# Linear attention's six projections as seven products of halves, x kept outside, states in a ring; one side of the FFN in two pieces

## The chip, the cores and the metric

The kernel runs on one core of a Trainium2 chip. TensorE (PE) multiplies: a stationary operand of 128 x 128 is loaded (PEld), a moving operand of up to 512 columns streams past it, and the sums land in PSUM. VectorE (DVE) and ScalarE (ACT) work on SBUF and PSUM, GpSimd (POOL) on SBUF; SyncE (SP) and POOL issue the transfers from and to HBM. Each engine works through its own queue in order. The metric is the device time of one execution in microseconds (us), the median of several runs.

## The reference, cut to what matters

A trunk of four layers on 512 rows of 1024 columns: S5, gated linear attention, differential attention, S5, each followed by an FFN. Everything is float32. The second layer's mixer:

```python
def gla_mixer(h, w_in, w_a2, b_a, norm_g, w_o):
    proj = h @ w_in
    q, k, v, g, a_lo = jnp.split(proj, [512, 1024, 2048, 3072], axis=-1)
    log_a = jax.nn.log_sigmoid(a_lo @ w_a2 + b_a) / 16
    cum = jnp.cumsum(log_a in chunks of 64, axis=2)
    tot = cum[:, :, -1]
    k_dec = k * jnp.exp(tot[:, :, None] - cum)
    upd = jnp.einsum('bnchk,bnchv->bnhkv', k_dec, v)
    state = exp(tot)[..., None] * state + upd        # over the 8 chunks, 4 heads
    o = jnp.einsum('bnchk,bnhkv->bnchv', q, states)
    o = o * rsqrt(mean(o * o) + eps) * norm_g        # per head
    return (o * silu(g)) @ w_o

x = x + gla_mixer(rmsnorm(x, norm_mix[1]), ...)
x = x + swiglu_ffn(rmsnorm(x, norm_ffn[1]), w_gate_up[1], w_down[1])
```

`q` and `k` have 512 columns each, `v` and `g` 1024 each, `a_lo` has 16. So `h @ w_in` is six blocks of 512 columns and a narrow one.

## The kernel before

**Products.** Each float32 product is made of three: an operand is split into a rounded high part and the low rest (`high`, a cast on ACT, L405; `low`, a subtraction on DVE, L413), and high x high, high x low and low x high are summed in PSUM (`mm3`, L433 to L435). A weight block is loaded by SP into one of three staging tiles (`wst`) and split into one of five tiles (`whl`).

**FFN blocks.** The gate and up products of the FFN already use seven products instead of eight (`seven_block`, `seven_product` with the matmul at L576). Rows of h are halved (th), its columns are halved (the depth), and a pair of 256-column weight blocks makes the 2 x 2 outputs. The left sides are 11, 12, 22 (quarters of h, transposed) and 1 to 4 (sums and differences of quarters); each lies split in `place`. The right sides are weight quarters 11, 21, 22 and sums of them: two sums are made by a load that adds to what is there (POOL, L612), two by an addition on DVE (L669). A product is 24 matmuls of 256 columns. The products are called one, five, six, two, seven, three, four; `a` and `c` are banks of the tag acc, `d` (product two) is one of the tag s.

**Sides.** `Sides` holds h for such a layer: the four quarters F in one tile, the sides 11 and 12 behind one another in another (L166 to L168, at 48 and 2112 of 4160 elements), the others opened in the layer's own pool. `Left` holds h split as a whole (`hT`), for layers that use plain products. Either is filled in the tail of the stage before: `take` multiplies x by the gain, `put` transposes, `keep` stores.

**The order.** `hand` says which engines follow the order in which the program is written; the others are ordered by a planner with a cost model, earliest written first among what it holds to be ready. An FFN begins with a start written out for all engines (`plan`, L755 to L770), in which two blocks run interleaved while the norm's factors and the sides are being made. The other blocks are the planner's. Linear attention has only TensorE written out.

**Linear attention before** (`gla`, L1894). q comes from `gemm_a4` (weights stationary, so that q is transposed). The low-rank gate (L1950) follows. Then five plain blocks by `gemm_b` (L437): v0, k, v1, g0, g1, each with four steps of 24 matmuls of 512 columns. Between the steps other work is put: `decays` (L1956: the gate's second product, and Abs, Exp, Ln on ACT), `later` (the suffix sums and their Exp into `kd`), `totals` (L1971), the recurrence `updates` and `readout` (L1986, L2013), and the transposes of the output (L2049). All eight states of two heads are kept in tiles of [128, 8, 256]. A readout takes squares on ACT and a root on POOL (L524). x stays in SBUF. The output projection (L2100) fills the next FFN's sides.

Of the kernel before, what the change touches and what calls it, by code (L numbers as in the profile page):

```python
# [22 lines left out]
P = 128  # L23
# [13 lines left out]
DIFF_LAYER = 2  # L37
LAMBDA_INIT = 0.8 - 0.6 * math.exp(-0.3 * DIFF_LAYER)

# [114 lines left out]
class Sides(Left):  # L154
# [5 lines left out]

    def room(self):
        F = self.tr.hp.tile([P, 4, 4, 256], F32, tag="hT", name="halves")
        self.whole = F
        self.F = {(0, 0): F[:, 0], (1, 0): F[:, 1], (0, 1): F[:, 2], (1, 1): F[:, 3]}

        two = self.tr.hp.tile([P, 4096 + 64], F32R, tag="hT", name="sides")  # L166
        at = lambda n: two[:, n : n + 2048].rearrange("p (z k n) -> p z k n", z=2, k=4)
        self.place = {"11": at(48), "12": at(2112)}  # L168
        self.heads = []

    def quarter(self, q, half, b):
        return self.w[
            q * 512 : (q + 1) * 512, half * FFN_HIDDEN + b * 256 : half * FFN_HIDDEN + (b + 1) * 256
        ].rearrange("(a p) n -> p a n", p=P)
# [15 lines left out]
    def parts(self, name, src, ks=slice(0, 4)):  # L190
        o = self.place[name][:, :, ks]
        self.tr.nc.scalar.copy(o[:, 0], src)
        self.tr.nc.vector.tensor_tensor(o[:, 1], src, o[:, 0].bitcast(F32), op=ALU.subtract)
# [132 lines left out]
class Trunk:  # L326
# [110 lines left out]
    def gemm_b(self, stat, w, nk, c0, evac, k0=0, tail=0, between=(), ahead=None, jobs=False, behind=None):  # L437
# [25 lines left out]
        if tail:  # L463
# [4 lines left out]
            for t in range(NT):  # L468
# [6 lines left out]
                evac(t, accs[t])  # L475

# [89 lines left out]
    def seven_product(self, side, w, bank, first, hl=None):  # L566
# [4 lines left out]
        for j in range(2):  # L571
            c = slice(j * P, (j + 1) * P)
            o = bank[:, j * 256 : (j + 1) * 256]
            for k in range(4):
                for n, (x, y) in enumerate(((0, 0), (0, 1), (1, 0))):
                    mm(  # L576
                        o, hl[:, x, k, c], side[:, y, k], start=first and not (j or k or n),
                        stop=k == 3 and n == 2, skip_group_check=True,
                    )

    def seven_block(self, fp, slots, left, wgu, b, turn, na):
# [4 lines left out]
        A = left.place  # L586
# [52 lines left out]
        def product(side, name, bank, first):  # L639
            self.seven_product(A[side], W.get(name), bank, first, H.pop(name, None))  # L640
# [81 lines left out]
    def ffn(self, l, left, after=None, turn=False, aside=None, small=None):  # L722
# [7 lines left out]
        with self.tc.tile_pool(name=f"ffn{l}", bufs=1, reuse_waits="tile") as fp:  # L730
# [40 lines left out]
            for step in plan.split():  # L771
                name, _, n = step.partition(":")
                if n:
                    f["ab".index(n)][name]()
                elif name[-1] in "ab":
                    word = next(w for w in ("split", "add", "high", "low") if name.startswith(w))
                    w = name[len(word) : -1]
                    f["ab".index(name[-1])][word]({"S": "1", "F": "1"}.get(w, w))
                elif name in ("finish", "diag", "spread", "rows"):
                    getattr(left, name)()  # L780
                elif name == "square":
                    left.square(NT - 1, 1)
                elif name == "flush":
                    self.flush()
                elif name == "turn":
                    r = self.turn_x(left.r) if turn else r
                else:
                    word = next(w for w in ("total", "high", "low") if name.startswith(w))
                    getattr(left, word)(name[len(word) :])
# [10 lines left out]
            for nb in (4, 4, 3) if na == 4 else (3, 3, 3, 2):  # L800
# [25 lines left out]
                if b0 + nb == 11:  # L826
                    nxt = (Chunks if turn else Last if l == 3 else Left)(self, after)
                for d in range(2):
                    tail = 4 if d == 1 and b0 + nb == 11 else 0
                    self.gemm_b(stat, wd, 2 * nb, d * 512, self.add_x(d, nxt, r), k0=2 * b0, tail=tail, jobs=jobs,  # L830
                                behind=None if d or l == 0 else dict(self.last))
# [1061 lines left out]

    def gla(self, l, left, after):  # L1894
# [4 lines left out]
        self.hand(mybir.EngineType.PE)  # L1899
        with self.tc.tile_pool(name="gla", bufs=1) as p:  # L1900
            self.edge(p, 64)
            big = lambda name, tag="g8", bufs=5: p.tile([P, 4, 512], F32, tag=tag, name=name, bufs=bufs)
            late = lambda name: big(name, "g8late", 3)
            oT = [p.tile([P, 2, 4, SEQ], F32R, name="oT0"), None]
            qT = late("qT")
            T = lambda tag, bufs=2: p.tile([P, 512], F32, tag=tag, name=tag, bufs=bufs)

            mask = p.tile([P, P], F32, name="mask")
# [7 lines left out]
            ind = p.tile([P, 2], F32, name="ind")  # L1916
# [3 lines left out]
            ng = p.tile([P, D], F32, name="ng")  # L1920
            nc.sync.dma_start(ng[:], i["gla_norm"][0].partition_broadcast(P))
            wa2 = p.tile([P, 512], F32, name="wa2")
            nc.gpsimd.memset(wa2[:], 0.0)
# [3 lines left out]
            wal = self.wp.tile([P, KT, 16], F32, tag="wst", name="wal", bufs=3)  # L1927
            nc.sync.dma_start(wal[:], w[:, 3072:3088].rearrange("(a p) n -> p a n", p=P))
            walr = p.tile([P, KT, 32], F32R, name="walr")
            nc.scalar.copy(walr[:, :, :16], wal[:])  # L1930
            v.tensor_tensor(walr[:, :, 16:], wal[:], walr[:, :, :16].bitcast(F32), op=ALU.subtract)

            hT = left.hT
# [606 lines left out]
```

## Time and profile before

| what | value |
|---|---|
| median of the 3 runs shown | 2264.95 us (2261.33 to 2266.5) |
| the profiled execution, time | 2264.01 us |
| its span, first to last instruction | 2262.1 us |
| TensorE clock granted, mean | 0.996 |
| linear attention's q begins, last plain block before the output projection ends | 579.8 us, 748.1 us |

The page lists, for groups of instructions, busy time, mean duration of one, and the idle time of the engine in front of them with what ended most of it. A stage row gives for a stretch of time how long each engine was busy. A wait row names who waited for whom, in us, how often, and the longest. In a timeline the first number is the start, the second the duration of what was merged into the row; matmuls overlap, so the time that one takes is read from start to start.

### The profile page before, as it was taken

To read this page: it belongs to the slowest core of one execution; us is meant where nothing else is said; L and a number is where in the kernel's file an instruction comes from. 1 tells how busy PE (TensorE), PEld (TensorE's weight loads), DVE (VectorE), ACT (ScalarE), POOL (GpSimd) and SP (SyncE) were. 2 spreads that over 40 slices of the span, in tenths; PEclk is the share of its full clock that TensorE was granted. 3 is DMA by queue.
4 is the path that set the end of the run, shared out by engine and by line. 5 is a ranking of instruction groups with operands and counts; after the bars stand their busy time and mean duration, and the time that the engine had idled before them with its cause. 6 is when DMAs were issued, how large, how long until landed. Compare 5 with 4: busy or idle time off the path is not lost.

```text
span 2262.1 us, 37360 instructions
## 1 busy us (share of the span) xinstructions
PE 2191.7 (97%) x14967; PEld 1963.9 (87%) x14967; DVE 1580.2 (70%) x2411; ACT 1111.5 (49%) x1773; POOL 317.9 (14%) x432
## 2 busy tenths in 40 slices
PE   6999999999999999999999999999999899999998
PEld 5888889989777799998988888989998788989997
DVE  9955878776535488776745676967766965957675
ACT  8534535444443365564435676644544234635443
POOL 4301141431000010100002231101000000101000
PEclk9999999999999999999999999999999999999999
DMA  4356666763322566765237465985641546766632
GB/s 89 65 170 167 172 159 176 173 172 100 106 76 74 149 158 178 180 172 154 94 137 149 100 152 138 237 212 134 174 99 50 153 146 155 198 160 161 165 75 75
DMA packets 295527, 319.92 MB, mean 141 GB/s; under 512 B 70141, under 2 KB 235289, under 8 KB 295226
## 3 DMA queue, kind: packets, MB, share of 16 engines
q1 hardware_dynamic: 232730, 235.79, 34.5%
q0 software_dynamic: 62624, 81.75, 19.5%
q8 instruction: 118, 1.93, 0.4%
q14 instruction: 55, 0.45, 0.1%
HBM read 285.62 MB, written 16.65 MB: 134 GB/s over the span
## 4 chain that ended last, share of the span: by engine, by line
PE 48%; DVE 3%; ACT 2%; issue 1%; DMA 1%; POOL 0%; DVEq 0%; POOLq 0%; ACTq 0%; SPq 0%
PE a L576 10%; PE acc L433 8%; PE acc L435 8%; PE acc L434 8%; PE c L576 5%; PE d L576 3%; PE y L1481 1%; PE op L2323 1%; PE s L2290 1%; DVE whl L413 1%; PE acc L2378 1%; ACT whl L405 1%; PE V L1445 1%; PE tp L116 0%; DMA wst<-in_ffn_w_gate_up_dram 0%
## 5 line engine op out<-in xcount | busy, mean ns | idle before, releaser
L413 DVE TENSOR_TENSOR whl<-wst,whl 128x1024 fp32r<-128x1024 f32 x272 | 331.6, 1223 | 276.9 <-ACT whl L405 276.2
L405 ACT CAST whl<-wst 128x1024 fp32r<-128x1024 f32 x272 | 284.6, 1051 | 339.7 <-PE acc L435 250.3
L576 PE MATMUL a<-side,whl 128*128 128x256 f32 x3168 | 383.9, 277 | 6.9 <-DVE whl L413 6.0
L576 PEld LDWEIGHTS a<-side,whl 128*128 128x128 f32 x3168 | 371.0, 188 | 9.2 <-DVE whl L413 6.7
L433 PE MATMUL acc<-whl,act 128*128 128x512 f32 x704 | 276.4, 393 | 1.7 <-DVE g L621 1.2
L434 PE MATMUL acc<-whl,act 128*128 128x512 f32 x704 | 275.0, 391 | 0.0
L435 PE MATMUL acc<-whl,act 128*128 128x512 f32 x704 | 274.9, 390 | 0.0
L576 PE MATMUL c<-side,whl 128*128 128x256 f32 x2112 | 255.2, 277 | 3.3 <-DVE whl L413 3.3
L576 PEld LDWEIGHTS c<-side,whl 128*128 128x128 f32 x2112 | 247.0, 188 | 4.2 <-DVE whl L413 4.1
L413 DVE TENSOR_TENSOR whl<-slot,whl 128x1024 fp32r<-128x1024 f32 x105 | 127.7, 1221 | 67.3 <-ACT whl L405 66.9
L433 PEld LDWEIGHTS acc<-whl,act 128*128 128x128 f32 x704 | 132.5, 188 | 30.8 <-DVE g L621 1.7
L435 PEld LDWEIGHTS acc<-whl,act 128*128 128x128 f32 x704 | 132.4, 188 | 27.6
L405 ACT CAST whl<-slot 128x1024 fp32r<-128x1024 f32 x105 | 110.0, 1052 | 92.5 <-PE acc L435 41.2
L434 PEld LDWEIGHTS acc<-whl,act 128*128 128x128 f32 x704 | 132.4, 188 | 26.4 <-issue 0.2
L576 PE MATMUL d<-sides,whl 128*128 128x256 f32 x1056 | 133.7, 283 | 2.5 <-ACT whl L405 2.5
L576 PEld LDWEIGHTS d<-sides,whl 128*128 128x128 f32 x1056 | 128.9, 191 | 3.3 <-ACT whl L405 3.3
L576 PE MATMUL a<-sides,whl 128*128 128x256 f32 x1056 | 129.3, 278 | 1.2 <-DVE whl L413 1.2
L433 PE MATMUL acc<-whl,hT 128*128 128x512 f32 x320 | 128.6, 402 | 0.0
L576 PEld LDWEIGHTS a<-sides,whl 128*128 128x128 f32 x1056 | 125.2, 188 | 2.4 <-DVE whl L413 1.4
L435 PE MATMUL acc<-whl,hT 128*128 128x512 f32 x320 | 125.3, 392 | 0.0
L434 PE MATMUL acc<-whl,hT 128*128 128x512 f32 x320 | 125.3, 391 | 0.0
L612 POOL DMA_DIRECT2D wst<-in_ffn_w_gate_up_dram x44 | 57.0, 1295 | 443.9 <-DMA wst<-in_ffn_w_gate_up_dram 222.7
(456 smaller groups left out, 3935.1 us busy)
## 6 DMA issues: line engine op xcount, KB each, us to landing
wst<-in_ffn_w_gate_up_dram SPq DMA_DIRECT2D x88, 512.0 KB, 4.6
wst<-in_ffn_w_down_dram SPq DMA_DIRECT2D x88, 512.0 KB, 4.4
slot<-in_ffn_w_gate_up_dram SPq DMA_DIRECT2D x69, 512.0 KB, 5.7
wst<-in_ffn_w_gate_up_dram POOLq DMA_DIRECT2D x44, 512.0 KB, 6.2
halves<-in_ffn_w_gate_up_dram SPq DMA_DIRECT2D x42, 512.0 KB, 5.0
wst<-in_s_w_glu_dram SPq DMA_DIRECT2D x32, 512.0 KB, 4.9
wst<-in_gla_w_in_dram SPq DMA_DIRECT2D x24, 512.0 KB, 3.7
wst<-in_diff_w_qkv_dram SPq DMA_DIRECT2D x24, 512.0 KB, 4.6
```

What stands on the lines that cost most here:

```text
L405: self.last["high"] = self.nc.scalar.copy(hl[:, 0], w[:])
L413: self.last["low"] = self.nc.vector.tensor_tensor(hl[:, 1], w[:], hl[:, 0].bitcast(F32), op=ALU.subtract)
L433: mm(out, lh, rh, start=first, stop=False)
L434: mm(out, lh, rl, start=False, stop=False)
L435: self.last["mm"] = mm(out, ll, rh, start=False, stop=last)
L576: mm(o, hl[:, x, k, c], side[:, y, k], start=first and not (j or k or n), stop=k == 3 and n == 2, skip_group_check=True,)
L612: nc.gpsimd.dma_start(w[:], left.quarter(*plus, b), accum_op=ALU.add)
L1445: mm(V[kk][z][:, bs(b)], inm[:, z, bs(b)], U[:, bs(b)], start=True, stop=True)
L1481: mm(yb[:, b], q[:, j, b], om[:, j // 2, bs(b)], start=False, stop=j == 3)
L2290: nc.tensor.matmul(ss[m][:], qs[:, m, ts], ks[:, m, z], start=z == 0, stop=z == 1)
L2323: nc.tensor.matmul(op[:, 0], aT[:, kt], vall[0][:, kt, j * P : (j + 1) * P], start=kt == 0, stop=kt == 3)
L2378: nc.tensor.matmul(o, stat(k, x, t), hl[:, y, a], start=not (k or t % 2 or n), stop=k == KT - 1 and n == 2, skip_group_check=True,)
```

## The change

All six projections of the linear attention become blocks of seven products. `GLA_COLS` names the first 256 of each block's columns: the order is now q, v0, k, v1, g0, g1, and a pair is the two halves of one block. The layer's h is a `Sides` with its own columns.

- The FFN 0 tail now prepares the sides, two split weights and total 3 (`gla_ahead`, `middle`), all engines in written order; the first half of x is stored to HBM there, the second at the start of the layer, both by POOL.
- q and v0 run as an interleaved start with the FFN's plan, less its gate steps and with `gates` (the narrow weight) and `negative` (the factors with the sign changed). q is made with weights stationary; the others with `held`, where the side is stationary and the weight moves, so rows come out as rows. Their evacuation is in pieces of 256 columns, scaled by the norm's factor.
- The low-rank gate uses sides 11, 12, 1 and 22.
- k, v1, g0, g1 follow as `block`, seven steps each: `decays` after the first product of k, `totals` after the third, `later` after the first of v1, the recurrence of heads 0 and 1 in v1, that of 2 and 3 in g0, the transposes of the first output half in g1.
- The tile of x serves as `work`: the low-rank gate, a ring of three pairs of states, and scratch. After the last readout x is loaded back by POOL.
- `later` writes its Exp to scratch and multiplies it into `kd` on DVE; silu works in place on the gate.
- In `Sides`, for all layers, 11 moves to 560, and 12 is held as k = 0 at 0 and k = 1 to 3 at 2608, each split by its own two instructions.

```diff
+GLA_COLS = (0, 1024, 512, 1536, 2048, 2560)
...
-        at = lambda n: two[:, n : n + 2048].rearrange("p (z k n) -> p z k n", z=2, k=4)
-        self.place = {"11": at(48), "12": at(2112)}
+        at = lambda n, k=4: two[:, n : n + 512 * k].rearrange("p (z k n) -> p z k n", z=2, k=k)
+        self.place = {"11": at(560)}
+        self.split12 = [(slice(0, 1), at(0, 1)), (slice(1, 4), at(2608, 3))]
...
+        pieces = self.split12 if name == "12" else [(slice(0, 4), self.place[name])]
+        for ks, o in pieces:
+            self.tr.nc.scalar.copy(o[:, 0], src[:, ks])
+        for ks, o in pieces:
+            self.tr.nc.vector.tensor_tensor(o[:, 1], src[:, ks], o[:, 0].bitcast(F32), op=ALU.subtract)
...
+                    two = (row(x, k)[:, c], hl[:, y, k]) if held else (hl[:, x, k, c], row(y, k))
...
                     if l == 0:
+                        nxt = Sides(self, after, None, i["gla_w_in"][0], lambda half, b: GLA_COLS[b] + half * 256)
...
+    def gla_ahead(self, left):
+        self.xkept = self.dp.tile([SEQ, D], F32, name="xgla")
+        left.ahead(2)
+        self.nc.gpsimd.dma_start(
+            self.xkept[:].rearrange("(t p) c -> p t c", p=P)[:, :, :512], self.x[:, :, :512]
+        )
...
+            nf = self.sp.tile([P, NT], F32, name="nf", bufs=1)
...
+            nc.gpsimd.dma_start(xd[:, :, 512:], self.x[:, :, 512:])
...
+            plan = """
+                split21a one:a split21b square flush one:b total1 one_out:a finish high1 low1 total2 split1a high2 low2
+                negative one_out:b two:a two:b split1b high3 two_out:a five:a add22a highSa two_out:b lowSa five_out:a
+                five:b add22b highSb diag lowSb low3 split3a six:a spread five_out:b rows six:b six_out:a split3b seven:a
+                six_out:b total4 split22a high4 low4 seven:b seven_out:a split22b three:a seven_out:b gates
+                add21a high22 low22 three:b highFa add21b lowFa highFb lowFb four:a four:b three_out:a three_out:b
+                four_out:a four_out:b
+            """
...
+            work = self.xp.tile([P, NT, D], F32, tag="x", name="work")
+            flat = whole(work)
+            aT, wa2 = flat[:, :512], flat[:, 512:1024]
+            ring = flat[:, :3072].rearrange("p (s z c n) -> p s z c n", s=3, z=2, c=2)
...
                 for t, bank in enumerate(four("suf")):
                     nc.tensor.matmul(row(bank), mask[:], la[:, t], start=True, stop=True)
-                    nc.scalar.activation(kd[:, t], row(bank), AF.Exp, scale=1.0 / 16.0)
+                    e = T()
+                    nc.scalar.activation(e, row(bank), AF.Exp, scale=1.0 / 16.0)
+                    v.tensor_tensor(kd[:, t], kd[:, t], e, op=ALU.mult)
...
+            def block(b, out, between):
+                between = iter(between)
+                s = self.seven_quarters(slots, left, b, True, out, self.acc)
+                for y in ("direct", "room1", "room22", "room21", "summed"):
+                    s[y]()
+                def step(*names):
+                    for n in names:
+                        s[n]()
+                    next(between, lambda: None)()
+                step("one", "one_out")
+                step("five", "five_out")
+                s["add"]("22")
+                step("six", "six_out")
+                step("two", "two_out")
+                step("seven", "seven_out")
+                step("three", "three_out")
+                s["add"]("21")
+                step("four", "four_out")
...
             pause = lambda: None
-            values(0, (decays, pause, pause, later))
-            self.gemm_b(stat, w, KT, 512, evac_k, between=(totals,))
-            values(1, core(0))
...
-            gated(0, core(1))
...
-            gated(1, (first, *(lambda t=t: turned(0, (t,)) for t in (1, 2, 3))))
+            block(2, Rows(kd), (decays, pause, totals))
+            vs[1] = room("D", "v1")
+            block(3, Rows(vs[1]), (later, *core(0)))
+            block(4, gated(0, room("C", "gate0")), core(1))
+            self.x = self.xp.tile([P, NT, D], F32, tag="x", name="x")
+            nc.gpsimd.dma_start(self.x[:], xd)
+            oT = [[room("D", "oT0"), room("A", "oT0")], None]
+            turns = [pause] + [lambda t=t: turned(0, (t,)) for t in range(NT)]
+            block(5, gated(1, room("C", "gate1")), turns)
```

373 lines of the change are left out of this document (256 added, 117 removed).

## The prediction

> **What bounds the kernel now.** I read the page first (busy time, the costliest groups), then TensorE's waits and the busy time by stage around the linear attention, then the timeline of TensorE, ScalarE and VectorE there.
>
> ```profile
> span 2262.1 us, 37360 instructions
> PE 2191.7 (97%) x14967; PEld 1963.9 (87%) x14967; DVE 1580.2 (70%) x2411; ACT 1111.5 (49%) x1773; POOL 317.9 (14%) x432
> L576 PE MATMUL a<-side,whl 128*128 128x256 f32 x3168 | 383.9, 277 | 6.9 <-DVE whl L413 6.0
> L576 PE MATMUL d<-sides,whl 128*128 128x256 f32 x1056 | 133.7, 283 | 2.5 <-ACT whl L405 2.5
> ```
> ```profile
> 580.00:800.00 220.00, 218.24 (x1038) 169.88 (x1037) 94.85 (x150) 86.08 (x141) 13.15 (x20) 0.99 0.36 101
> 800.00:870.00 70.00, 66.67 (x574) 65.86 (x573) 65.65 (x76) 45.24 (x60) 8.78 (x7) 1.00 0.73 187
> 870.00:1110.00 240.00, 239.55 (x1690) 222.91 (x1689) 181.09 (x292) 128.28 (x182) 19.92 (x20) 1.00 0.57 151
> ```
> ```profile
> PE acc L435 <- DVE oT L530: 1.0, 2, 0.7
> PE tp L116 <- DVE hh L94: 0.8, 1, 0.8
> ```
> ```profile
> PE a L576 <- DVE whl L413: 1.7, 1, 1.7
> PE c L576 <- DVE whl L413: 1.1, 1, 1.1
> PE d L576 <- ACT whl L405: 0.4, 1, 0.4
> ```
>
> The stage rows give wall time, then busy time of PE, its weight loads, DVE, ACT and POOL. Linear attention fills 580 to 800: TensorE stands only 1.8 us, in the output projection (first list of waits), while DVE works 94.85 of 220 us. So only fewer TensorE cycles can shorten this stage, and DVE has room to pay for them. The next FFN shows the price: its first two blocks of seven products (800 to 870) keep DVE at 65.65 of 70 us, and TensorE waits 3.3 us for split weights (second list). After that, with DVE at 181.09 of 240, nothing waits.
>
> **1. The products.** Starts on TensorE:
>
> ```profile
> 540.99 2.88 PE L576 MATMUL a<-side,whl 128*128 128x256 f32 x24
> 543.71 3.02 PE L576 MATMUL d<-sides,whl 128*128 128x256 f32 x24
> 546.57 2.90 PE L576 MATMUL a<-side,whl 128*128 128x256 f32 x24
> ...
> 597.66 0.39 PE L433 MATMUL any<-hT,whl 128*128 128x512 f32 x1
> ...
> 600.38 0.39 PE L433 MATMUL any<-hT,whl 128*128 128x512 f32 x1
> ```
>
> Twelve 512-wide matmuls take 600.38 - 597.66 = 2.72 us, one 0.2267. A product of 24 matmuls of 256 columns takes 543.71 - 540.99 = 2.72 too. A projection was 96 matmuls of 512, 21.8 us; it becomes 7 products, 19.0. Six of them: 130.6 - 114.2 = **-16.3 us**. (The gate's low-rank product goes from 16 matmuls of 512 to 32 of 256: nothing.) Were each second product to run like d (2.86), 0.8 less is gained.
>
> **2. The written-out start (q and the first values).** It is the FFN's order of steps, so I price it by that start's 3.3 us. Against it: the gate's scaling and the activations' splits are gone, and the low-rank product follows, which asks nothing of DVE; so the second and third waits should fall away. For a loss: the FFN 0 tail ahead of it is only 48 matmuls (10.9 us), in which DVE must now also split two weights ahead and form total 3. **+2.5 us**, ends 1.5 and 6.
>
> **3. The wait at the totals.** This is where I expect the gain to leak.
>
> ```profile
> 613.39 0.59 ACT L1961 ACTIVATE e<-z 128x512 f32<-128x512 f32 x1
> 614.00 1.28 ACT L1962 ACT_TABLE_LOAD   x1
> 615.29 0.63 ACT L1962 ACTIVATE e<-e 128x512 f32<-128x512 f32 x1
> ...
> 629.07 1.28 ACT L1963 ACT_TABLE_LOAD   x1
> 630.36 0.63 ACT L1963 ACTIVATE e<-e 128x512 f32<-128x512 f32 x1
> 630.90 1.98 ACT L405 CAST whl<-wst 128x1024 fp32r<-128x1024 f32 x2
> ```
> ```profile
> 631.02 0.69 DVE L1964 SCALAR_TENSOR_TENSOR la<-z,e 128x512 f32<-128x512 f32 x1 [3.20 <-ACT e L1963]
> ```
> ```profile
> 612.20 3.60 PE L1959 MATMUL z<-wa,aT 128*128 128x512 f32 x8
> 615.23 0.80 PE L433 MATMUL acc<-whl,hT 128*128 128x512 f32 x1
> ...
> 640.89 3.73 PE L1975 MATMUL dps<-ind,la 128*128 128x2 f32 x32
> 644.48 0.78 PE L433 MATMUL acc<-whl,hT 128*128 128x512 f32 x1
> ```
>
> The decays' last `la` is done at 631.71, 19.5 us after their matmuls begin (612.20). Before, the totals (L1975) came 28.7 us after that beginning. In the new order, written out for TensorE, the decays stand behind the first product of the keys' block, and the totals two products later: 615.23 - 612.20 = 3.0 us of decays, five 2.72, six 2.72, so 8.5. The totals take 644.48 - 640.89 = 3.6 us, tile by tile, and without a wait would end at 12.1. Their last quarter (0.9) cannot start before 19.5 and ends at 20.4: a wait of 8.3. One cast of 1.05 us (two in 1.98 at 630.90) that the planner slips between the exponentials adds itself: **+9 us**. What is queued behind the chain on ScalarE is the cast of six's weight, and the products after it. At most five split weights can be held, now 5 x 2.72 = 13.6 us of work, where each covered 5.44 before. Ends: 0 (decays finished in time) and 16 (six's cast behind the whole chain: chain 18.8, cast 1.05, low part 1.22, six 2.72, totals 3.6 = 27.4, and 1 of restart, less 12.1). The row at 644.48 shows that the first product after the totals starts slowly; it does so in both kernels, so nothing is added.
>
> A page speaks against this place: the Trainium skill, ScalarE: Activation LUTs, section "What ACT_TABLE_LOAD costs", puts 1.38 us of drain behind each 1.283 us load. By it the chain's eight loads would take 11 us more and the change would lose. Here the next activation starts at 615.29, where the load of 614.00 ends, so I give the rule no weight.
>
> **4. The three blocks with the recurrence.** DVE, per block: seven low parts, two sums of weights, six half-width evacuations, and the recurrence, the key decay, the gate's product or the splits of the turned output.
>
> ```profile
> L413 DVE TENSOR_TENSOR whl<-wst,whl 128x1024 fp32r<-128x1024 f32 x31 | 37.9, 1224 | 80.7 <-ACT whl L405 80.7
> L2008 DVE SCALAR_TENSOR_TENSOR st<-st,dec,upd 128x256 f32<-128x256 f32 x28 | 12.2, 475 | 0.0
> L2036 DVE SCALAR_TENSOR_TENSOR on<-op,rs,ng 128x256 f32<-128x256 f32 x16 | 7.0, 480 | 3.1 <-POOL rs L524 3.1
> L2061 DVE TENSOR_TENSOR on<-on,e 128x512 f32<-128x512 f32 x8 | 5.3, 688 | 4.4 <-ACT e L2060 4.3
> L530 DVE TENSOR_TENSOR oT<-oTp,oT 128x512 fp32r<-128x512 f32 x8 | 5.3, 683 | 0.1
> ```
> ```profile
> 667.95 1.14 PE L1998 MATMUL upd<-v,kd 64*128 64x256 f32 x8
> 669.02 0.50 PE L433 MATMUL acc<-whl,hT 128*128 128x512 f32 x1
> ...
> 674.68 1.08 PE L2022 MATMUL op<-st,qT 128*64 128x256 f32 x8
> 675.70 1.14 PE L1998 MATMUL upd<-v,kd 64*128 64x256 f32 x8
> ```
>
> Low parts and sums are 9 x 1.22 = 11.0, evacuations 6 x 0.48 = 2.9, a recurrence 16 x 0.475 + 8 x 0.48 + small = 12, the rest 4 x 0.69 = 2.8. Values block: 28.7 us of DVE against 19.0 + 3.0 (the suffix sums, of the decays' form) + 4 x (1.07 + 1.02) = 30.4 of TensorE. First gate block: 28.7 against 27.4. Second: 11.0 + 2.9 + 2.8 + 2.7 = 19.4 against 20.5. Together 76.8 against 78.3. Where DVE set the pace (800 to 870) it was busy 94%; 76.8 / 0.94 = 81.7, so **+3 us**; ends 0 (five weights split ahead in the wait of part 3) and 15 (the rival below).
>
> **5. Side 12 in two pieces.** In the FFNs the product of side 12 (d) takes 546.57 - 543.71 = 2.86 us, all others 2.72. The page's means, 283 and 277 ns, say so for all 1056 of d's matmuls, 44 products. Every one of its 24 matmuls starts about 6 ns late, so this is no wait, and the place of the side is what differs. If both pieces run like the other sides: 44 x 0.14 = 6.2 us won. Three of the four k land exactly 2048 elements behind side 11, which is fast; of the fourth I know nothing. **-4.7 us** (three quarters); ends -6.2 and +6.2, as side 11 moves too and could catch d's pace. The two extra instructions per side (an extra start on ACT and DVE) lie in the tail of the stage before: nothing.
>
> **6. x outside.** The two stores stand on POOL's queue ahead of the start and behind its loads; the work tile needs them some 40 us later (14 products of 2.72 and the low-rank product).
>
> ```profile
> xkeep<-x POOLq DMA_DIRECT2D x1, 2048.0 KB, 12.0
> ```
>
> A store of all of x landed in 12.0 us. The way back begins when the last readout frees the tile, and the first sum into x comes after the last gate block (20.5) and most of the first output half (21.8): hidden, 12 if that cover were gone. SP's and POOL's loads of the last block are issued beside it. States in a ring of three, qT's scaling and silu apart: same operations, DVE time counted above. The 1.8 us of waits in the output projection stay.
>
> **Sum:** -16.3 + 2.5 + 9 + 3 - 4.7 = -6.5. The profiled execution took 2264.0 us (span 2262.1 and 1.9 around it), 0.9 under the median 2264.95 of the runs shown. 2264.0 - 6.5 = **2257.5 us**.
>
> **Rivals.**
> *POOL's queue paces DVE (slower).* POOL computes the readouts' roots; before, it had nothing else in those blocks, and DVE still waited 3.1 us for it (L2036). Now each block puts two accumulating loads into the same queue.
>
> ```profile
> L612 POOL DMA_DIRECT2D wst<-in_ffn_w_gate_up_dram x44 | 57.0, 1295 | 443.9 <-DMA wst<-in_ffn_w_gate_up_dram 222.7
> ```
>
> In the FFNs POOL stood before 44 of these 443.9 us, 10 us each, half of it on the plain load's landing. A root behind one stops DVE's queue, and with it the low parts that TensorE wants. Four of the eight readouts held 5 us each, less the 1.5 that is spare each time: +14, 2271.5. It decides once DVE waits over 11 us for POOL there. Against: the planner may put roots first.
>
> *The totals do not wait* (decays early enough, or the planner groups the loads): -9, 2248.5. Against: 17.6 us of ScalarE chain are in the trace.
>
> *Side 12 does not do what it says* (pieces as slow as before): 2262.2.
>
> **Chances.** Forecast 0.43 (2251 to 2262 by its own terms), POOL's queue or six's cast behind the chain, with a saturated DVE, 0.25, no wait at the totals 0.17, side 12 without effect 0.15. The range takes in the second and third: 2246 to 2271. A measurement of this kernel tells about 0.2%, 4.5 us, from no change. Faster: 0.40 of the forecast, 0.17 of no wait, 0.01 of side 12 = 0.58; same: 0.03 of the forecast, 0.12 of side 12, 0.03 of POOL's queue = 0.18; slower: 0.22 of POOL's queue, 0.02 of side 12 = 0.24.
>
> **What would show it.** Right: products at 2.72 us in the attention; a wait at L1975's totals of 8 to 10 us behind `la`; DVE above 90% from the values block on, with TensorE's waits there under 5 us; d in the FFNs nearer 2.72 than 2.86. Wrong: a totals wait under 3 or over 12; waits of DVE for POOL's roots above 11 us; other side products slower than 2.72 (their addresses may shift by a small new tile); x's return named before a sum into x.

## The result, and the profile after

| kernel | median | lowest to highest |
|---|---|---|
| before | 2263.14 us | 2261.04 to 2266.5 |
| after | 2290.1 us | 2288.71 to 2292.56 |

After to before: 1.0114, 95% interval 1.0102 to 1.0126. The forecast was 2257.5 us, range 2246 to 2271: 32.6 us too low, and on the wrong side.

The page of the kernel after (span, busy time, groups: busy us, mean ns of one, idle before):

```profile
span 2287.0 us, 38452 instructions
PE 2214.7 (97%) x15415; PEld 1998.0 (87%) x15415; DVE 1638.5 (72%) x2487; ACT 1143.8 (50%) x1837; POOL 340.1 (15%) x447
L592 PE MATMUL a<-side,whl 128*128 128x256 f32 x3240 | 406.4, 281 | 6.9 <-DVE whl L426 4.4
L447 PE MATMUL acc<-whl,act 128*128 128x512 f32 x704 | 279.3, 397 | 0.0
L592 PE MATMUL c<-side,whl 128*128 128x256 f32 x2160 | 270.1, 281 | 2.8 <-DVE whl L426 2.8
L592 PE MATMUL d<-sides,whl 128*128 128x256 f32 x1080 | 132.5, 278 | 2.6 <-ACT whl L418 2.6
```

The groups of TensorE before, where the prediction did not show them:

```profile
L434 PE MATMUL acc<-whl,act 128*128 128x512 f32 x704 | 275.0, 391 | 0.0
L576 PE MATMUL c<-side,whl 128*128 128x256 f32 x2112 | 255.2, 277 | 3.3 <-DVE whl L413 3.3
```

TensorE is as busy as before (97%), and the waits for VectorE's split weights in front of the products on the opened sides have become smaller (4.4 and 2.8 us, for 6.0 and 3.3). The FFNs' matmuls themselves are slower: products on the opened sides 281 ns for 277, the FFN's output matmuls 397 for 391. Only d gained (278 for 283). The timelines of one group of products show it, first before, then after (start, duration of the merged row). A group is the run of products between two output stretches, and an output stretch is the run of the FFN's output matmuls behind it.

```profile
419.20 2.99 PE L576 MATMUL a<-sides,whl 128*128 128x256 f32 x24
422.02 2.99 PE L576 MATMUL c<-side,whl 128*128 128x256 f32 x24
424.85 2.99 PE L576 MATMUL a<-side,whl 128*128 128x256 f32 x24
427.68 3.04 PE L576 MATMUL d<-sides,whl 128*128 128x256 f32 x24
430.55 2.90 PE L576 MATMUL a<-side,whl 128*128 128x256 f32 x24
```
```profile
420.80 2.90 PE L592 MATMUL a<-sides,whl 128*128 128x256 f32 x24
423.54 3.00 PE L592 MATMUL c<-side,whl 128*128 128x256 f32 x24
426.38 3.00 PE L592 MATMUL a<-side,whl 128*128 128x256 f32 x24
429.22 2.94 PE L592 MATMUL d<-sides,whl 128*128 128x256 f32 x24
431.99 3.00 PE L592 MATMUL a<-side,whl 128*128 128x256 f32 x24
```

Start to start, before: 2.82, 2.83, 2.83, 2.87, and behind these nearly all 2.72, product d aside (2.86). After: 2.74, 2.84, 2.84, 2.77, 2.83, and this pattern repeats to the end of the group. The three blocks of this group (21 products) take 57.93 us before (419.20 to the first output matmul at 477.13) and 59.13 after (420.80 to 479.93); an output stretch of FFN 2 takes 43.54 and 44.81. Summed over the four FFNs, from the first start of each stretch to the first of the next, the groups of products cost 16.8 us more and the output stretches 10.8 more. Together that is 27.6 us; less the 2.7 that the linear attention gained (below), it is the 24.9 us by which the spans of the two profiles differ.

The linear attention gained. From its first product to the first output matmul: 168.24 us before (579.83 to 748.07), 165.51 after (584.49 to 750.00). TensorE's longest waits there (total, times, longest), and VectorE's wait for POOL's roots:

```profile
PE dps L2229 <- DVE la L2216: 3.6, 1, 3.6
PE op L2269 <- DVE work L2256: 0.9, 2, 0.7
```
```profile
DVE on L2283 <- POOL rs L539: 3.9, 7, 1.1
```

The gain is 2.7 us where some 2 were forecast for the attention's terms, and the longest wait left there is the one for the last decay.

### The profile page after: what moved, and what is told of

The parts are those of the page before. It is cut to its first block, busy times and chain, and to the rows that moved or that the text cites. A ratio compares the mean times of both kernels' runs of the same rounds, so it can differ in the third digit from the quotient of the medians.

```text
span 2287.0 us, 38452 instructions
## 1 busy us (share of the span) xinstructions
PE 2214.7 (97%) x15415; PEld 1998.0 (87%) x15415; DVE 1638.5 (72%) x2487; ACT 1143.8 (50%) x1837; POOL 340.1 (15%) x447
## 4 chain that ended last, share of the span: by engine, by line
PE 83%; DVE 7%; ACT 5%; issue 2%; DMA 1%; SPq 1%; POOL 0%; DVEq 0%; ACTq 0%; POOLq 0%
PE a L592 20%; PE acc L446 12%; PE acc L448 12%; PE acc L447 12%; PE c L592 10%; PE d L592 5%; PE y L1618 2%; DVE whl L426 2%; ACT whl L418 1%; PE op L2571 1%; PE V L1582 1%; PE s L2538 1%; PE tp L117 1%; PE acc L2626 1%; DMA wst<-in_ffn_w_down_dram 1%
## 5 line engine op out<-in xcount | busy, mean ns | idle before, releaser
L426 DVE TENSOR_TENSOR whl<-wst,whl 128x1024 fp32r<-128x1024 f32 x260 | 317.2, 1224 | 227.7 <-ACT whl L418 225.8
L592 PE MATMUL a<-side,whl 128*128 128x256 f32 x3240 | 406.4, 281 | 6.9 <-DVE whl L426 4.4
L418 ACT CAST whl<-wst 128x1024 fp32r<-128x1024 f32 x260 | 272.1, 1051 | 270.5 <-PE acc L448 179.7
L592 PEld LDWEIGHTS a<-side,whl 128*128 128x128 f32 x3240 | 392.1, 188 | 9.3 <-DVE whl L426 5.6
L446 PE MATMUL acc<-whl,act 128*128 128x512 f32 x704 | 280.8, 399 | 1.9 <-DVE g L766 1.9
L447 PE MATMUL acc<-whl,act 128*128 128x512 f32 x704 | 279.3, 397 | 0.0
L448 PE MATMUL acc<-whl,act 128*128 128x512 f32 x704 | 279.1, 396 | 0.0
L592 PE MATMUL c<-side,whl 128*128 128x256 f32 x2160 | 270.1, 281 | 2.8 <-DVE whl L426 2.8
L592 PEld LDWEIGHTS c<-side,whl 128*128 128x128 f32 x2160 | 261.3, 188 | 3.7 <-DVE whl L426 3.7
L447 PEld LDWEIGHTS acc<-whl,act 128*128 128x128 f32 x704 | 132.8, 189 | 30.3
L418 ACT CAST whl<-halves 128x1024 fp32r<-128x1024 f32 x87 | 91.3, 1051 | 91.1 <-DVE halves L815 32.1
L426 DVE TENSOR_TENSOR whl<-halves,whl 128x1024 fp32r<-128x1024 f32 x87 | 106.2, 1222 | 39.3 <-ACT whl L418 39.0
L859 ACT CAST act<-r 128x512 fp32r<-128x512 f32 (+1 forms) x110 | 66.3, 645 | 99.1 <-DVE r L840 83.3
```

The lines of the kernel that those rows point to most:

```text
L418: self.last["high"] = self.nc.scalar.copy(hl[:, 0], w[:])
L426: self.last["low"] = self.nc.vector.tensor_tensor(hl[:, 1], w[:], hl[:, 0].bitcast(F32), op=ALU.subtract)
L446: mm(out, lh, rh, start=first, stop=False)
L447: mm(out, lh, rl, start=False, stop=False)
L448: self.last["mm"] = mm(out, ll, rh, start=False, stop=last)
L592: mm(o, *two, start=first and not (j or k or n), stop=k == 3 and n == 2, skip_group_check=True,)
```

## The experiments

Medians are given with the ratio to the kernel before on the same chip; the medians of before lie between 2265.8 and 2267.8 us.

**Theory A** is the place of the operands, that is, the bytes at which the two operands of a matmul begin in SBUF. The change adds one small tile, `nf`, which takes 32 bytes, to a pool that stands ahead of the layers' pools, and they all begin 32 bytes later. From the built programs' memory maps (bytes within a partition):

```
                          before     after
split weights whl          63936     63936
tile of sides 11 and 12    30656     30656
side 1 (2, 3, 4, 22 alike) 132736    132768
act (FFN 0)               149184    149216
```

**Rival B** is the new program itself: its order, its waits, the two pieces, other traffic.

### e1 to e4: the place, or the program

e1 takes `nf` from the layer's own pool; e2 and e3 are the kernel before with 32 and 64 unused bytes in the small pool; e4 is the kernel before with side 12 in two pieces (the diff's edits of `Sides`) and nothing else.

```diff
 e1 (after)
-            nf = self.sp.tile([P, NT], F32, name="nf", bufs=1)
+            nf = p.tile([P, NT], F32, name="nf")
 e2 (before); e3 with [P, 16]
         self.sp = ep("small", 8)
+        self.sp.tile([P, 8], F32, name="pad", bufs=1)
```

> The changed kernel, with the 32 bytes of the negative factors taken out of the small pool and put at the end of the layer's own pool, so that the tiles of all layer pools lie where they lay before (opened sides at 0 instead of 32 past a multiple of 128 bytes, act at 64 instead of 96). Theory A, the place of the operands slows each matmul: FFN products back at 2.72 us, 512-wide output matmuls back at 0.227 us, time 2250 us (2244 to 2257). Rival B, the slower matmuls come with the new program itself: products stay at 2.84, time 2288 to 2291.

> The kernel before, with nothing but 32 unused bytes added to the small pool: all tiles of the layer pools lie 32 bytes further. Theory A: products on the opened sides 2.84, d stays 2.86, output matmuls 0.233, time 2293 us (2285 to 2303). Rival B: 2263 us.

> The kernel before with 64 unused bytes: opened sides at 64 past a multiple of 128, act at 0. If moving operands want multiples of 128 bytes: opened sides run like side 12 does, 2.86, and 5 x 44 x 0.14 = 31 us are lost, 2294 us, less what the output matmuls may win with act at 0. If multiples of 64 are enough: 2263 us, and side 12's pace has another cause. Rival B: 2263 us.

> The kernel before with the FFN's side 12 in two pieces alone, side 11 and the three larger parts of 12 at multiples of 128 bytes. Theory A: d 2.77, 44 x 0.09 = 4 us won, 2259 us. Rival: no effect, 2263 us.

Measured: e1 2259.63 us, 0.997 (0.996 to 0.9981). e2 2297.77, 1.0137 (1.0117 to 1.0156). e3 2304.05, 1.0165 (1.0147 to 1.0184). e4 2262.28, 0.9981 (0.9971 to 0.999). Groups of e2, then of e1:

```profile
L577 PE MATMUL a<-side,whl 128*128 128x256 f32 x3168 | 397.2, 281 | 5.0 <-DVE whl L414 4.4 <-ACT r L681 0.6
L435 PE MATMUL acc<-whl,act 128*128 128x512 f32 x704 | 279.1, 396 | 0.0
```
```profile
L592 PE MATMUL a<-side,whl 128*128 128x256 f32 x3240 | 392.5, 277 | 9.9 <-DVE whl L426 6.2
L447 PE MATMUL acc<-whl,act 128*128 128x512 f32 x704 | 274.4, 390 | 0.0
```

Thirty-two idle bytes give the kernel before the slow means of the kernel after, and cost 1.4%, 31 us. Moving one 32-byte tile gives the kernel after 277 and 390 ns back and makes it faster than before. B falls; the place is the cause of the loss. Two sizes were missed: e1 lies 2.6 us above the range given for theory A, and e3 is the slowest of the four, its output matmuls at 397 ns where they were thought to win.

### e5, e6, e9, e13: which rule the place follows

e5 and e6 move the split weights: together with the layer pools (e5), or against everything else (e6: weights down by 192 bytes, pools and sides 11 and 12 by 128, so that only the weights change their place within 128 bytes). e9 moves the pools by 128 and the weights by 256 bytes. e13 moves weights and pools by 128 together, and sides 11 and 12 with them.

```diff
 e5 (before)
         self.wp = ep("wp", 3)
+        self.wp.tile([P, 16], F32, name="pad", bufs=1)
 e6: as e5, and
-        two = self.tr.hp.tile([P, 4096 + 64], F32R, tag="hT", name="sides")
+        two = self.tr.hp.tile([P, 4096 + 32], F32R, tag="hT", name="sides")
-        self.place = {"11": at(48), "12": at(2112)}
+        self.place = {"11": at(16), "12": at(2080)}
+        self.sp.tile([P, 16], F32, name="pad2", bufs=1)
 e9: the shorter tile and places of e6, no pad in wp, and [P, 32] in the small pool
 e13: as e6's places with 4096 + 48, no pads
```

> The kernel before, with 64 unused bytes ahead of the split weights in their pool, so that the split weights, the staged weights and all layer pools behind them move by 64 bytes together; sides 11 and 12 stay. Theory A1 (what counts is how the two operands of a matmul lie to each other): the layer sides and the activations keep their distance to the split weights, so these products and the output matmuls keep 277 and 391 ns; side 11 and side 12 change roles (a<-sides 277 to about 283, d 283 to about 277), and the time stays at 2264 within 5 us. Theory A2 (only the side's and the activations' own place counts): as with 64 bytes in the small pool, 283 and 397 ns, and 2300 to 2308 us.

> The kernel before, with the split and the staged weights moved by 64 bytes and everything else left at its place in a line of 128 bytes (the sides' tile is 32 elements shorter, and 64 unused bytes follow in the small pool). Theory A1 (distance between the two operands): products on sides 1, 2, 3, 4, 22 and 11 go to about 283 ns, d to about 277, the output matmuls to about 397, and the time to some 2300 us. Theory A2 (own place of side and activations): 277, 283 and 391 ns as before, 2264 us within 4.

> The kernel before, with the sides' tile 32 elements shorter and 128 unused bytes in the small pool, so that the split weights move down by 256 bytes and all layer pools by 128, a move larger than any that cost time so far, but one that leaves every operand's place within a line of 128 bytes as it was. If the place within 128 bytes is what counts: 2264 us, products 277 and 283 (d) ns, output matmuls 391. If any move of the pools costs, or a longer line counts (256 bytes or more): 2290 or more.

> The kernel before with the sides' tile 16 elements shorter, so that the split weights and all layer pools move down by 128 bytes together, and sides 11 and 12 by 128 bytes inside their tile: every distance between the operands of the FFNs' matmuls is kept modulo 256 bytes. Only the turned inputs of the projections come to lie otherwise (64 and 128 bytes off instead of 0). Theory D (the distance modulo 256 counts): 277 ns for a and c, 283 for d, 391 for the output matmuls, and only the matmuls on hT and its like slower, by some 5 ns: 2264 to 2270. Theory M (any move costs): 2290 or more, 280 to 283 ns.

Measured: e5 2274.9 us, 1.0039 (1.0026 to 1.0053). e6 2311.52, 1.02 (1.0184 to 1.0216). e9 2302.1, 1.015 (1.0137 to 1.0163). e13 2274.39, 1.0036 (1.0024 to 1.0049). The time of e5 is 9 us above before, where it was expected within 5; the next part comes back to it. In its groups sides 11 and 12 changed roles, as theory A1 said (what counts is how the two operands of a matmul lie to each other):

```profile
L577 PE MATMUL a<-side,whl 128*128 128x256 f32 x3168 | 386.8, 278 | 6.2 <-DVE whl L414 6.0
L577 PE MATMUL a<-sides,whl 128*128 128x256 f32 x1056 | 133.7, 283 | 1.6 <-DVE whl L414 1.2 <-DVE x L560 0.5
L577 PE MATMUL d<-sides,whl 128*128 128x256 f32 x1056 | 129.2, 278 | 2.5 <-ACT whl L406 2.5
```

So an operand's own place does not count, but its distance from the other operand. My first guess, the place within 128 bytes, fell with e9: nothing changed modulo 128, and it was slow. The rule that fits these means is the distance from the split weights modulo 256. It is worked out from the memory maps, as start of side or act minus start of `whl`; before, 132736 - 63936 = 68800, which leaves 192.

| kernel | sides 1 to 4, 22 | act | a, c | output (L447 or its like) |
|---|---|---|---|---|
| before, e1 | 192 | 0 | 277 ns | 390, 391 ns |
| e5, e13 | 192 | 0 | 277, 278 | 390, 391 |
| after, e2 | 224 | 32 | 281 | 396, 397 |
| e3, e6 | 0 | 64 | 283 | 397 |
| e9 | 64 | 128 | 280 | 395 |

In e6, e9 and e13 side 1 begins at the same 132608 and `act` at the same 149056. Only the weights begin elsewhere, at 63744, 63680 and 63808, and the matmuls on the opened sides took 283, 280 and 277 to 278 ns. e13 was the test of this rule, and its groups came out as foretold, d included:

```profile
L576 PE MATMUL a<-side,whl 128*128 128x256 f32 x3168 | 385.4, 278 | 5.9 <-DVE whl L413 4.4 <-ACT r L680 0.8 <-ACT r L648 0.4
L434 PE MATMUL acc<-whl,act 128*128 128x512 f32 x704 | 274.5, 390 | 0.0
L576 PE MATMUL d<-sides,whl 128*128 128x256 f32 x1056 | 133.6, 283 | 2.5 <-ACT whl L405 2.5
L433 PE MATMUL acc<-whl,hT 128*128 128x512 f32 x320 | 131.0, 409 | 0.0
```

Its time is 0.36% above before all the same, over the 2264 to 2270 us expected. The operands whose distance it did change are slower: hT here 409 (402 before), and zT of the S5 layers 395 (390) in 768 matmuls, some 4 us. Why d was slow before is told by the same rule: side 12 lay at 30656 + 4 x 2112 = 39104, a distance of 0, and side 11 at 192.

### e7, e10, e11, e14, e16: the first quarter of side 12

In the new `Sides` three quarters of 12 (k = 1 to 3), and all of 11, lie at 192 and the first quarter of 12 (k = 0) at 0. These runs move that quarter: to 64 (e10; e7 with 64 bytes ahead of the attention's pool besides), to 192 like the rest (e14), or give side 11 such a quarter too (e16). e11 (on e8, below) was meant as e16, under the modulo-128 guess, and put six quarters at 64 instead.

```diff
 e1's line, and its first place in e10 and e7, in e14
-        self.split12 = [(slice(0, 1), at(0, 1)), (slice(1, 4), at(2608, 3))]
+        self.split12 = [(slice(0, 1), at(16, 1)), (slice(1, 4), at(2608, 3))]
+        self.split12 = [(slice(0, 1), at(48, 1)), (slice(1, 4), at(2608, 3))]
 e7 besides, ahead of the attention's tiles
+            self.edge(p, 64)
 e16; e11 with 1040 and 2576
+        cut = lambda a, c: [(slice(0, 1), at(a, 1)), (slice(1, 4), at(c, 3))]
+        self.split = {"11": cut(0, 1072), "12": cut(512, 2608)}
```

> The kernel after with the negated scales in the layer's pool (which was 2259.6), an edge of 64 bytes ahead of the linear attention's own pool, and the first quarter of side 12 on a start of 64 bytes instead of 0. Theory A1 (distance): in the linear attention the 25 products that hold a side of the layer's pool as the stationary operand, with the split weights moving, go from 2.83 to 2.72 (2.7 us less), the five or so of the first block the other way (0.6 more), the output projection gains up to 1, and d goes from 2.76 to 2.72 (44 products, 1.6 us less): 2255 us. Theory A2, with held products slow for another reason: only d's 1.6 us, 2258.

> The kernel after with the negated scales in the layer's pool (2259.6 us), and the first quarter of side 12 started at 64 bytes in place of 0, so that all of sides 11 and 12 lie at the start of a line of 128 bytes. Run e7, which had this and the 64 bytes ahead of the linear attention, was slower in the FFNs, where whole groups of products ran at 2.83 us instead of 2.72. Theory P (a slow pace, once entered behind an output matmul, lasts until a matmul with an operand at another place ends it; the quarter at byte 0 was that matmul): 2268 to 2274, with groups of products at 2.83. Theory Q (the 64 bytes ahead of the linear attention did it): 2258, d at 2.72.

> Run e8 (2257.5 us) with side 11 split as side 12 is, its first quarter also 64 bytes off the start of a line and its other three at the start. Theory P: the slow pace, which now lasts for the first three products of most groups, ends in the first product; some 14 groups by two or three products by 0.11 us, 3 to 5 us less: 2253. Theory Q, or no part of side 11 at another place helps: a few matmuls more at the slow place, 2258 to 2262.

> The kernel after with the negated scales in the layer's pool (e1, 2259.6 us), and the first quarter of side 12 started at element 48 in place of 0, so that now every side lies 192 bytes from the split weights modulo 256. Theory D alone (each matmul by its own distance): d at 277 instead of 278 ns, 2258. Theory P (the slow pace behind an output matmul ends only in a product at another distance): nothing ends it any more, whole groups at 2.83 us, 2270 to 2285.

> e1 (2259.6 us) with side 11 split as side 12 is: the first quarters of both at distance 0 from the split weights modulo 256, the other three of both at 192. Theory P: the first product of each group then ends the slow pace that now lasts for three products, so some 14 groups gain two or three times 0.11 us: 2255 to 2257. If the first quarter's distance does not end it: 2260 or a little more for the matmuls at distance 0.

Measured: e7 2274.2 us, 1.0041 (1.0028 to 1.0053). e10 2276.95, 1.0037 (1.0024 to 1.005). e11 2283.74, 1.0067 (1.0055 to 1.0079). e14 2276.8, 1.0042 (1.0028 to 1.0056). e16 2259.51, 0.9967 (0.9956 to 0.9979). e7 and e11 are 16 us and more above all that had been expected of them, and e10 is 3 us above. The same group of products in e14, then in e16:

```profile
419.24 2.99 PE L592 MATMUL a<-sides,whl 128*128 128x256 f32 x24
422.07 2.99 PE L592 MATMUL c<-side,whl 128*128 128x256 f32 x24
...
427.72 2.99 PE L592 MATMUL d<-sides,whl 128*128 128x256 f32 x24
430.55 2.99 PE L592 MATMUL a<-side,whl 128*128 128x256 f32 x24
433.38 2.99 PE L592 MATMUL c<-side,whl 128*128 128x256 f32 x24
```
```profile
417.74 2.93 PE L593 MATMUL a<-sides,whl 128*128 128x256 f32 x24
420.51 2.88 PE L593 MATMUL c<-side,whl 128*128 128x256 f32 x24
423.23 2.88 PE L593 MATMUL a<-side,whl 128*128 128x256 f32 x24
425.95 2.92 PE L593 MATMUL d<-sides,whl 128*128 128x256 f32 x24
```

With every side at the good distance, 192, e14 is slow: each product takes 2.83 us to the end of the group, and so it is in most groups (the first blocks of the FFN behind the linear attention ran at 2.72). So there are two paces, that is, two times from one product's start to the next, at one and the same distance. A group mostly enters the slow one behind an output stretch, and matmuls at distance 0 end it: all of d in the timeline of before, a quarter of the first product in e16. That quarter costs some 0.05 us itself (417.74 to 420.51 is 2.77). At 64 it ends nothing in most groups (e10). The gain of e16 over e1 foreseen from this shows in the groups of products (some 2 us less in all), but its median is e1's: 3 us are within what two medians of these kernels differ by.

Two runs limit this account. In e11 the first quarters of 11 and 12 lie at 0 too, but the other three at 64, and the products on sides 1 to 4 and 22, all at 192, stay at 2.82 to 2.83 nearly everywhere:

```profile
422.30 3.01 PE L593 MATMUL a<-sides,whl 128*128 128x256 f32 x24
425.15 2.99 PE L593 MATMUL c<-side,whl 128*128 128x256 f32 x24
427.97 2.99 PE L593 MATMUL a<-side,whl 128*128 128x256 f32 x24
430.80 3.01 PE L593 MATMUL d<-sides,whl 128*128 128x256 f32 x24
```

In e5 side 11 lies at 128, and behind its product the pace changes to and fro: in the group that begins at 420.83 the six products behind the first one take 2.72 to 2.74, the six behind the next one 2.82 to 2.83. Its groups of products take 4 to 5 us more than before in all, about half of the 9 us that were not foreseen. How the paces follow from the places is therefore known in part only.

### e8, e12, e17, e18: the wait at the totals

The timeline of TensorE after, and the granted clock there (the number behind the five engines' busy times, 0.74):

```profile
638.69 2.96 PE L592 MATMUL a<-whl,side 128*128 128x256 f32 x24
641.49 1.84 PE L2229 MATMUL dps<-ind,la 128*128 128x2 f32 x16
646.97 3.57 PE L2229 MATMUL dps<-ind,la 128*128 128x2 f32 x16 [3.64 <-DVE la L2216]
650.40 5.19 PE L592 MATMUL d<-whl,sides 128*128 128x256 f32 x24
655.42 2.99 PE L592 MATMUL a<-whl,side 128*128 128x256 f32 x24
```
```profile
640.00:650.00 10.00, 6.36 (x46) 6.28 (x44) 3.67 (x5) 9.92 (x15) 1.28 (x1) 0.74 0.48 95
```

The wait is 3.6 us, and the clock takes as much again: the totals last 8.9 less the wait, 5.3, where 3.6 were enough before, and d takes 5.0 where its like take 2.8. e8 asks for the totals two products later; e12 reads the keys out on VectorE besides; e17 is e8's edit on e16; e18 is e17 with the decays in two halves and the totals one product later still.

```diff
 e8, e12, e17
-            block(2, Rows(kd), (decays, pause, totals))
+            block(2, Rows(kd), (decays, pause, pause, pause, totals))
 e12 besides, in Rows.copy where the rows are kd's
-                        nc.scalar.mul(o, y, fac[:, t : t + 1])
+                        v.tensor_scalar_mul(o, y, fac[:, t : t + 1])
 e18
+            block(2, Rows(kd), (lambda: decays((0, 1)), pause, lambda: decays((2, 3)), pause, pause, totals))
```

> The kernel after with the negated scales in the layer's pool, and the totals of the decays asked for two products later in the keys' block, behind product seven instead of product six. The wait for the last decay was 3.7 us, and the first product behind it took 4.7 us in place of 2.8 at a lowered clock. If the wait is real and nothing else is late behind it: both go, 5.6 us less, 2254. If the time goes to the next wait (split weights, or the clock that is lowered there anyway): 2257 to 2260.

> Run e8 (2257.5 us) with the keys' products read out by VectorE instead of ScalarE. In e8 the totals no longer waited, but product six waited 3.5 us for a readout of keys that stood on ScalarE behind the exponentials, and TensorE's granted clock fell to 0.74 behind that wait, which cost some 3 to 5 us more. If that readout is all that hangs behind the exponentials: wait and lowered clock go, 2250 to 2253. If the next split weight is late instead: 2255 to 2258.

> e16 (both sides in two pieces, the negated scales in the layer's pool; 2259.5 us) with the totals behind product seven, as in e8. If the two gains add: 2255 to 2257. If e8's difference from e1 was only the spread between runs, since the wait was passed on to the keys' readout: 2259.

> e17 with the decays in two halves, the first behind product one as before, the second behind product six, and the totals behind product three, so that the keys' readouts stand between the two halves of ScalarE's chain. If the chain being in one piece was what held the readout and, through it, TensorE: the wait of 3.5 us and the lowered clock behind it (3 to 5 us) mostly go, 2250 to 2254. If the next split weight is late instead, behind the second half: a wait of 2 to 4 us for it, 2256 to 2259.

Measured: e8 2257.51 us, 0.9966 (0.9953 to 0.9978). e12 2260.45, 0.9972 (0.996 to 0.9983). e17 2257.04, 0.9957 (0.9944 to 0.9969). e18 2256.23, 0.9952 (0.9939 to 0.9966). e12 is slower than both times expected of it. e18 lies where a late split weight had been expected, but the only such wait was 0.2 us. The longest wait of the attention in e8 (e17 has the same), in e12, and in e18 (its transposes aside):

```profile
PE a L592 <- ACT kd L2100: 3.5, 1, 3.5
```
```profile
PE a L592 <- DVE kd L2102: 4.6, 1, 4.6
```
```profile
PE op L2270 <- DVE work L2257: 0.7, 1, 0.7
PE a L593 <- DVE kd L2105: 0.5, 1, 0.5
```

A step moved behind a late chain passes its wait on. In e8 product seven needs the bank of six, whose readout stands on ScalarE behind the exponentials; in e12 it stands on VectorE behind `la`, which waits for the same exponentials. Only breaking the chain (e18) removed the long wait; from first product to output projection the attention then takes 162.3 us (577.07 to 739.37) for 164.9 in e1 (581.06 to 746.00). In e8 it takes 165.8, so the lower median of e8 does not come from there. Even in e18 the product behind the totals took 5.0 us, with waits of only 0.4 and 0.5 us around it. In the kernel before, TensorE did not wait at the totals at all and was busy throughout, and the granted clock was 0.83 over these 10 us all the same:

```profile
640.00:650.00 10.00, 10.00 (x55) 8.74 (x54) 1.23 (x1) 1.24 (x2) 0.00 (x0) 0.83 0.23 72
```

So the 32 matmuls of two columns go with a lowered clock even without a long wait. The medians of e17 and e18 differ by less than their intervals. The trace's dips agree in part with the Trainium skill, TensorE: Matmul & The Clock Gate, section "HAM oscillation — how this bites in real kernels", whose abstract rule is no idle gap over some 3.4 us. The wait of 3.6 us fits it; in e18 and in the kernel before, the clock also fell around very small matmuls with gaps of 0.5 us or none.

### e15: held products at the mirrored distance

```diff
 e1, ahead of the attention's tiles
+            self.edge(p, 128)
```

> e1 (2259.6 us) with an edge of 128 bytes ahead of the linear attention's own pool, so that its sides lie 64 bytes from the split weights in place of 192. There the split weights move and the side is held, the other way round, so by theory D the good distance is the mirrored one, 256 - 192 = 64: held products on these sides from 2.83 to 2.72, 25 of them, 2.7 us less; the first block's, not held, 0.6 more; the output projection between -1 and +1: 2257. If the mirrored distance is not the good one: 2.83 to 2.88 as in e7, 2260 to 2262.

Measured: 2261.34 us, 0.9974 (0.9964 to 0.9984). The attention takes 165.2 us (577.75 to 742.99): nothing gained. Held and other products ran there partly at 2.72, partly at 2.83. What the held products need is open.

## Why the prediction was wrong

1. **The step that failed** is none of the six terms. It is the cost of `nf`, to which the sum gave nothing: the last part named "other side products slower than 2.72 (their addresses may shift by a small new tile)" as a sign of error, but there was no term for it, no end of the range and no chance. It cost some 31 us in the kernel before (e2), and about as much in the kernel after (its ratio less that of e1 is 1.44%, some 33 us). The trace held the warning: I read from d that "the place of the side is what differs", and applied that to side 12 alone, not to every operand that the new tile moves. In term 5 I let the loss reach +6.2, by side 11, with five other sides and the activations left out.
2. **Products (-16.3): right in kind, too large.** 41 recorded products of the attention take 121.1 us after, 2.95 each, not 2.72. Without the clock's 2.2 us in d that is 7 us less gain. Held products run at 2.80 to 2.83, and at 2.9 to 3.3 where other work stands between them (in the timeline above 638.69 to 641.49 is 2.80, 655.42 is followed by 658.25). e1 has the same, so this is not the 32 bytes.
3. **Start (+2.5): 0.** TensorE waits for no split weight there in the kernel after.
4. **Totals (+9): near.** 3.6 of wait and 3.9 of lowered clock, less the 1.6 that a lowered clock cost before too (eight matmuls from 644.48 to 647.89, 3.4 us for 1.8): 5.9. I had the wait too long (ScalarE ran the exponentials in pairs, with four table loads for eight) and the clock at nothing.
5. **Recurrence (+3): 0.9**, VectorE busy 77% (49.0 of 64 us from 666 to 730), not above 90%. The term had also counted 16 state updates per block, where its own row has 28 for two blocks; that is 1 us of VectorE.
6. **Side 12 (-4.7): right.** e4 gives 0.19% (0.10 to 0.29), some 4 us; d went to 278 ns.
7. **x outside (0): right.** No wait names its return.

Terms 1 to 4 for the attention: -9 + 0 + 5.9 + 0.9 = -2.2, against a measured -2.7. So the forecast for the program (-6.5) was met by e1 (0.3%, 6.7 us), but by luck: the products won some 7 us less than forecast, and the start, the totals and the recurrence cost some 8 less. The 32 bytes turned it over. e1's ratio less e4's is 0.11%, 2.5 us, which agrees with the attention's share, though each of the two ratios is only known to 0.1%. POOL's queue did not become a bound: VectorE waited 3.9 us for its roots where that rival needed 11.

## What to carry to other kernels

When a change adds or resizes a tile, list what lies behind it, and compare the distances between the operands of the hottest matmuls before pricing anything else. Where two groups of one shape differ by a few ns per matmul without a wait, that difference is a price that any layout change can put on all groups. A wait behind a long chain isn't cured by asking later: look for what else stands behind that chain, and break it.

## What the runs showed of the hardware

- A distance of 192 modulo 256 bytes between side and split weights (0 for the FFN's activations) gave 277 and 391 ns, as long as other matmuls ended the slow pace (279 to 281 in e14, where none did). The sides at 0, 64 or 224 gave 280 to 283, the activations at 32, 64 or 128 gave 395 to 399. For 64 this is one run of the FFNs (e9), at 2.83 us per product; in e15 a product with its side at 64 ran at 2.72 once (601.86 to 604.58). The Trainium skill, SBUF — State Buffer, section "Operand start alignment", lets an fp32 operand start at any multiple of four bytes and says that this is about legality, not speed; the runs show the speed to differ. Whether 256 is the whole period was not separated from larger ones, and what in the chip makes it so stays open.
- At the good distance there are two paces, 2.72 and 2.83 us per product, and a few matmuls at distance 0 lead from the slow to the fast one (e14 against e16), though not in e11. Why is open too.
- The lowest median of all runs is that of e18, 0.9952 of before, not separated from e17's 0.9957. It keeps the whole change, with `nf` in the layer's pool, both sides in two pieces and the decays in two halves.
